# A residual turned partly by 32x32 blocks on VectorE and a gather through DRAM, partly on TensorE

## The chip, the cores and the metric

The kernel runs on one core of a Trainium2 chip. The metric is the device time of one execution in microseconds (us), the median of the runs. Beside it there is one profiled execution, with a trace of every instruction; its span runs from the first instruction of the program to the last. In the views of the profile PE is TensorE, PEld its weight loads, DVE is VectorE, ACT is ScalarE, POOL is GpSimd and SP is SyncE, which here only issues transfers.

## What is computed

One layer of a transformer trunk over 512 tokens of width 2048, in float32. With the depth of 1 only the sliding-window attention mixer is used:

```python
hn = rmsnorm(x, norm_g[0])
y = swa_mixer(hn, swa_w_in[0], swa_w_out[0], swa_sinks[0], rel_bias)   # ends in (out * silu(gate)) @ w_out
x = x + y
emb = p[0] @ ple_proj[0]
g = sigmoid(rmsnorm(x, ple_norm[0]) @ ple_gate[0])
x = x + emb * g
return rmsnorm(x, final_g)
```

Two matrix products of 512x2048 by 2048x2048 matter here: the **output projection** by `w_out`, whose result is added to x, and the **gate product** by `ple_gate`, which takes that new x as its left factor. Between the two, x must be turned: the output projection leaves it with tokens on the 128 partitions, and the gate product needs it with features on the partitions.

## The kernel before

**Number format and pieces.** Every float32 product is made of three passes: each operand is split in a high part (`hi`) and a rest (`lo`) of a narrower type, and `mm3` (lines 126 to 128) issues hi*hi, lo*hi and hi*lo. The weights come in pieces of 128x1024. For each piece SP issues the load of `braw` (line 752), ScalarE casts `bhi` (line 760) and VectorE subtracts to get `blo` (line 761). `Pieces.ahead` splits a piece when TensorE begins on the one two places before it, and the buffers for the split parts are three, so the cast of a piece waits until TensorE has finished the piece three places before it.

**Stages and units.** Each of the two products is done by a scheme of block products that needs fewer multiplications, in six units p, in the order 1, 7, 6, 5, 3, 4, each for two column halves jj. `unit` goes over four pieces m = 0 to 3 of a unit; a piece is 12 matmuls. After each piece come, in this order, some of the list `later` (additions to x, `add_to_x`, lines 1054 and 1056), the calls of `todo` (a step, named (p, jj, m) below), and `between`, which may put the two pieces of a "small" product of 6 matmuls each in between. The last unit of the output projection, p = 4, has small pieces after every step but the last two, two of them after step (4, 1, 0).

**The residual.** `x1[j][:, t, :]` is column block j (of 512) of token block t (of 128). Column blocks 2 and 3 are complete for tokens 256 to 511 after unit 5 and for tokens 0 to 255 after unit 3; column blocks 0 and 1 are complete for tokens 0 to 255 during unit 4 and for tokens 256 to 511 after it.

**The turns.** `turn(kp, th, tag)` turns two of the 16 feature chunks for half of the tokens: four TensorE transposes of 128x128 into one bank of PSUM (line 1038), then two ScalarE multiplications by the norm's weights that write `hT` (line 1041). There are 16 calls, so 64 transposes. Twelve of them stand in the steps of unit 4: 1, 2, 2 and 2 calls in the steps of its first half, and 0, 1, 2 and 2 in those of its second. The first eight (chunks 8 to 15, that is column blocks 2 and 3) take up the first half and step (4, 1, 1). Four more stand in the four steps of (1, 0), the first unit of the gate product.

**The gate product's first operands.** `ple_first`, the forms of unit 1, is four split pairs (lines 865 and 866) of column blocks 2 and 3 for tokens 0 to 255, one made in each step of (4, 1). The forms of unit 7 (lines 858, 870 and 871) also take tokens 256 to 511 of those blocks.

**What sets the order.** In this part of the kernel only TensorE and SP run in the order in which the program is written. VectorE, ScalarE and GpSimd each run in an order that a planner makes when the program is built, from its own costs and from what is ready; it may pull an instruction ahead of its place in the program. From the second unit of the gate product on, all five run in written order. Each engine takes its instructions in its order, one after the other, and waits at one whose input is not there.

**Other names.** `fg` holds the last norm's weights for all partitions (1 MB in SBUF); its load is issued by SP after unit 3 (line 1350). `s1` and `s7` are buffers of 128x2048 that the embedding's products use until step (3, 0, 0) and the gate product from its second half unit on. The tag `e` has two buffers of 128x1024, used by the embedding before and by its loads later.

Of the kernel before, what the change touches and what calls it, by code (L numbers as in the profile page):

```python
# [11 lines left out]
F32 = mybir.dt.float32  # L12
# [6 lines left out]
D = 2048  # L19
S = 512  # L20
P = 128
# [34 lines left out]
def trunk_kernel(ctx: ExitStack, tc: tile.TileContext, a: dict):  # L56
    nc = tc.nc

    def pool(name, bufs=1, **kw):
        return ctx.enter_context(tc.tile_pool(name=name, bufs=bufs, **kw))  # L60
# [9 lines left out]
    pn = const.tile([P, KC], F32, name="pn")  # L70
# [8 lines left out]
    def quarter(name):  # L79
        return whole.tile([P, 4, S], F32, tag="quarter", name=name)  # L80
# [5 lines left out]
    WE = 1024  # L86
# [71 lines left out]
    def run(gen):  # L158
        for _ in gen:
            pass  # L160
# [38 lines left out]
    for k in range(KC):  # L199
# [7 lines left out]
        both = start_pool.tile([P, 2 * 768], F32R, tag="w0s", name=f"w0s{k}")  # L207
# [46 lines left out]
        else:  # L254
            high()
            if k == 1:
                src = xw[:, w_at[512] : w_at[512] + 256]
# [9 lines left out]
        f, e = k == 0, k == KC - 1  # L267
# [18 lines left out]
        for part in "hl" if f else "lh":  # L286
            for t in range(NB):
                c = slice(t * P, (t + 1) * P)
# [6 lines left out]
        if 3 <= k < 3 + NB:  # L295
            t = k - 3
# [104 lines left out]
    for b in range(exact, BUCKETS):  # L401
        d = np.nonzero(bk == b)[0]
        if len(d):
            lo, n = P - 1 + int(d.min()), len(d)
# [301 lines left out]
    for nm, p in SUMS:  # L706
        for q in (6, 5) if (nm, p) == ("ple_gate", 5) else (p,):
            sum_small(nm, q)
        for jj in range(2):
            for m in range(4):  # L710
                t = summed[nm, p, jj, m] = tc.dram_tile([P, WE], F32, name=f"{nm}_{p}_{jj}_{m}")
# [194 lines left out]
    blocks = TWOS * UNITS  # L906
# [64 lines left out]
    late = pool("late", reuse_waits="tile")  # L971
    rooms.append(late)
    x1s = late.tile([P, 4, NB, 512], F32, name="x1s")
    x1 = [x1s[:, j] for j in range(4)]
# [15 lines left out]
    later = []  # L990
# [6 lines left out]
    def unit(p, jj, at, forms, todo, between=lambda m, ps: None):  # L997

        ps = banks(p, jj, forms.nm)
        f = forms.made[p]  # L1000
        first = p not in (6, 5, 3)
        for m in range(4):
            bh, bl = B.get(at[p, jj][m])
            for kk in range(2):
                k = 2 * m + kk
                fh, fl = f[m]
                for tb in range(2):
                    mm3(ps[tb], fh[:, kk, blk(tb)], fl[:, kk, blk(tb)], bh[kk], bl[kk], first and k == 0, k == 7, not first)
            some_later(4 - m)
            todo()  # L1010
            between(m, ps)
        return ps


    def load_x(j, queue):
        queue.dma_start(x1[j], a["x"].rearrange("(t p) d -> p t d", p=P)[:, :, j * 512 : (j + 1) * 512])

    def partial(nm):
        return late.tile([P, 2, 2, 512], F32, tag="partial", name=nm, bufs=3)

    s1, s2, s7 = partial("s1"), partial("s2"), partial("s7")
# [4 lines left out]
    hT, swapped = {}, {}  # L1026

    def turn(kp, th, tag):
# [10 lines left out]
        for n in range(2):  # L1039
            k = 2 * kp + n  # L1040
            nc.scalar.mul(hT[g][:, k % 4, th * 256 : th * 256 + 256], tp[:, n * 256 : n * 256 + 256], pn[:, k : k + 1])

    ple_forms = Forms(swapped, "g")
    ple_first = ple_forms.steps(1)


    missing = {(j, t): {(0, 0): 1, (1, 0): 3, (0, 1): 1, (1, 1): 2}[t // 2, j // 2] for j in range(4) for t in range(NB)}
# [255 lines left out]
    turns = []  # L1303
# [3 lines left out]
    x_at = {(1, 0, 3): 2, (1, 1, 1): 1, (7, 0, 0): 3}  # L1307
    waiting = {(7, 0): (1, 0), (6, 0): (1, 1)}
    held = {}
    for n, p in enumerate(ORDER_OUT):  # L1310
        nxt = out_forms.steps(ORDER_OUT[n + 1]) if n < 5 else iter(())
        for jj in range(2):
            later.extend(held.pop(waiting.get((p, jj)), ()))
            calls = iter(range(4))

            def between(m, ps):
                if (p, jj, m) in EMBED_AT:
                    embedding.slot()
                q = small_steps.get((p, jj, m))
                if q is not None:  # L1320
                    small_out.prepare(q)
                for q in SMALL["w_out"].get((p, jj), {}).get(m, ()):
                    small_out.product(q)

            def todo():
                step = next(calls)
                part = x_at.get((p, jj, step))
                if part is not None:
                    load_x(part, nc.sync)
                part = embed_steps.get((p, jj, step))  # L1330
                if part is not None:
                    embedding.prepare(part)
                next(nxt, None)
                if p == 4:

                    for _ in range({0: 1, 1: 2, 2: 2, 3: 2, 5: 1, 6: 2, 7: 2}.get(4 * jj + step, 0)):
                        turn(*turns.pop(0), "o")
                    if jj:
                        next(ple_first, None)

            ps = unit(p, jj, at_out, out_forms, todo, between)
            posts = [partial_of(add_y, p, jj, tb, ps[tb]) for tb in range(2)]
            if p == 1:
                held[p, jj] = posts
            else:
                later.extend(posts)
        run(nxt)
        if p == 3:
            fg = late.tile([P, D], F32, tag="fg", name="fg")
            nc.sync.dma_start(fg, a["final_g"].partition_broadcast(P))  # L1350
        if p == 3:
            turns = [(kp, th) for kp0, th in ((4, 1), (4, 0), (0, 0)) for kp in range(kp0, kp0 + 4)]
    run(ple_first)
    assert not turns

# [18 lines left out]
    def load_embeds(c, jj):  # L1374
        t = embed_of[c, jj] = late.tile([P, 2, 512], F32, tag="e", name=f"e{c}_{jj}", bufs=2)
        nc.sync.dma_start(t, embeds[c, jj])

    def embeds_for(of, which):
        return {t: embed_of[of, which][:, t % 2] for t in ((2, 3) if of == 5 else (0, 1))}
# [47 lines left out]
    turns = [(kp, 1) for kp in range(4)]  # L1427
# [70 lines left out]
    for n, p in enumerate(ORDER_PLE[:-1]):  # L1498
        if n == 1:

            ctx.enter_context(
                tc.manual_schedule(
                    engines={getattr(mybir.EngineType, v) for v in ("PE", "SP", "DVE", "Activation", "Pool")}
                )
            )
        nxt = ple_forms.steps(ORDER_PLE[n + 1])
        for jj in range(2):
            calls = iter(range(4))

            def todo():  # L1510
                step = next(calls)
                k = early.get((p, jj, step))
                if (p, jj, step) in embed_loads:
                    load_embeds(*embed_loads[p, jj, step])
                while small_due:
                    small_due.pop(0)()
                if (p, jj, step) == (5, 0, 2):
                    assert len(moves) == 4
                    while moves:
                        moves.pop(0)()  # L1520
                if (p, jj, step) == (5, 0, 3):
                    for square in moved.pop(0):
                        square()
                if turns:
                    turn(*turns.pop(0), "t")
                    if not turns:
                        nc.vector.tensor_reduce(ss2, ssq2, axis=AX.X, op=ALU.add)
                        run(power_of_mean(rstd2, ss2, "r2"))
                        nc.scalar.activation(ss2[:, :1], ss2[:, :1], AF.Sigmoid)
                    return  # L1530
                next(nxt, None)
                if p == 1:
                    next(nxt, None)
                if k is not None:
                    split_last(k)
                if (p, jj, step) in opens:
                    open_bank(*opens[p, jj, step])

            def between(m, ps):
                if (p, m) == (7, 3):  # L1540
                    gate(p, jj, ps, None)
                q = ple_steps.get((p, jj, m))
                if q is not None:
                    small_ple.prepare(q)
                for q in SMALL["ple_gate"].get((p, jj), {}).get(m, ()):
                    small_ple.product(q)
                if (p, jj, m) == (6, 1, 1):
                    later.append(partial_of(gate_later, "sum", 0, None, embeds_for(1, 0)))

            ps = unit(p, jj, at_ple, ple_forms, todo, between)  # L1550
            last_two, held_e = (p, jj) == (3, 1), {}
            if not (p == 7 or last_two):
                later.insert(0, partial_of(gate_later, p, jj, ps, held_e))
            for of, which in EMBEDS.get((p, jj), ()):
                e = embeds_for(of, which)
                held_e.update(e)
                if of == 1:
                    later.insert(1, partial_of(gate_later, "sum", which, None, dict(e)))
                    held_e.clear()
            if p == 5:  # L1560
                while moved:
                    later.extend(moved.pop(0))
        run(nxt)
# [4 lines left out]
    f = ple_forms.made[4]  # L1568
# [84 lines left out]
    n = done[3]  # L1653
# [81 lines left out]
```

## Time and profile before

| | |
|---|---|
| median of 3 runs | 787.09 us (786.91 to 787.52) |
| the profiled execution | 787.18 us |
| its span | 785.5 us |
| TensorE clock granted, mean | 0.996 |
| output projection's unit 4, first half | 587.9 to 607.4 us of the span |
| its second half | 607.4 to 624.8 us |
| gate product's first half unit | 624.8 to about 637.9 us |

The table puts the stages by the first TensorE instruction of each in the trace. The profiled execution took 0.09 us more than the median, and 1.7 us of it lie outside the span. A row of a timeline begins with the start and the duration in us, then engine, line, operation, output and inputs; a row of a group ends with the count, the busy time in us, the mean duration of one in ns, and the idle time of the engine before it with what ended it.

### The profile page before, as it was taken

Reading aid. Unit: us, or ns where it says so; the run is one execution under the profiler, and the core shown is the slowest. Engines: PE = TensorE matmul, PEld = TensorE weight load, DVE = VectorE, ACT = ScalarE, POOL = GpSimd, SP = SyncE. Lnnn points to the kernel's source line nnn. Section 1 sums busy time; section 2 is a strip of 40 time slices with the busy share of each in tenths; the row PEclk is TensorE's granted clock in tenths of the full one; section 3 lists DMA queues with packets and bytes.
Section 4 is the critical chain, followed back from the end, with each engine's and each line's share of the span. In section 5 each row is a group of like instructions: output and inputs, shape, how many; then the busy total and the mean of one; then the engine's idle time right before and its main releaser. Section 6 shows DMA issues by size and latency. Waiting matters only on the chain.

```text
span 785.5 us, 11181 instructions
## 1 busy us (share of the span) xinstructions
PE 775.9 (99%) x3700; PEld 648.8 (83%) x3700; DVE 612.1 (78%) x1057; ACT 528.9 (67%) x1121; POOL 149.7 (19%) x273
## 2 busy tenths in 40 slices
PE   9999999999999999999999999999999999999995
PEld 7888888888888888888888888888888888888885
DVE  4547697877877688877878899976897958998996
ACT  6743586766767676766666655678778976667874
POOL 0201423122222314132322200001000002221111
PEclk9999999999999999999999999999999999999998
DMA  9988989999999989999997489868698179999956
GB/s 341 297 210 295 190 251 311 309 287 262 277 265 266 273 235 297 252 302 251 294 252 207 141 318 324 281 204 292 238 374 297 58 298 280 276 280 310 301 116 214
DMA packets 50393, 206.72 MB, mean 263 GB/s; under 512 B 7504, under 2 KB 8528, under 8 KB 44576
## 3 DMA queue, kind: packets, MB, share of 16 engines
q1 hardware_dynamic: 39152, 154.58, 54.9%
q0 software_dynamic: 11184, 51.44, 32.3%
q8 instruction: 29, 0.48, 0.3%
q14 instruction: 28, 0.23, 0.1%
HBM read 192.31 MB, written 75.55 MB: 341 GB/s over the span
## 4 chain that ended last, share of the span: by engine, by line
PE 97%; issue 1%; DMA 0%; DVE 0%; POOL 0%; POOLq 0%; ACT 0%; DVEq 0%; SPq 0%
PE gps L126 7%; PE gps L127 7%; PE gps L128 7%; PE qps L126 7%; PE qps L128 7%; PE qps L127 7%; PE o L127 6%; PE o L128 6%; PE o L126 6%; PE g L128 5%; PE g L127 5%; PE g L126 5%; PE s L485 2%; PE vps L290 2%; PE o L603 2%; PE pt L551 2%
## 5 line engine op out<-in xcount | busy, mean ns | idle before, releaser
L761 DVE TENSOR_TENSOR blo<-braw,bhi 128x1024 fp32r<-128x1024 f32 x100 | 121.9, 1222 | 30.7 <-ACT bhi L760 29.8
L760 ACT CAST bhi<-braw 128x1024 fp32r<-128x1024 f32 x100 | 105.0, 1050 | 39.1 <-PE o L128 15.1
L126 PE MATMUL gps<-xh,whi 128*128 128x512 f32 x256 | 100.0, 390 | 0.0
L127 PE MATMUL gps<-xl,whi 128*128 128x512 f32 x256 | 100.0, 390 | 0.0
L128 PE MATMUL gps<-xh,wlo 128*128 128x512 f32 x256 | 99.8, 390 | 0.0
L126 PE MATMUL qps<-xh,whi 128*128 128x512 f32 x224 | 87.8, 392 | 0.0
L128 PE MATMUL qps<-xh,wlo 128*128 128x512 f32 x224 | 87.5, 390 | 0.0
L127 PE MATMUL qps<-xl,whi 128*128 128x512 f32 x224 | 87.4, 390 | 0.0
L575 POOL TENSOR_SCALAR_AFFINE_SELECT own<-r 64x512 fp32r<-64x512 f32 (+1 forms) x48 | 32.4, 675 | 238.9 <-DVE r L565 235.7
L110 DVE TENSOR_TENSOR wlo<-wraw,whi 128x1024 fp32r<-128x1024 f32 x60 | 73.5, 1227 | 3.4 <-ACT whi L109 3.3
L127 PE MATMUL o<-blo,fho 128*128 128x512 f32 x192 | 74.8, 390 | 0.0
L126 PE MATMUL o<-bhi,fho 128*128 128x512 f32 x192 | 74.8, 390 | 0.0
L128 PE MATMUL o<-bhi,flo 128*128 128x512 f32 x192 | 74.8, 389 | 0.0
L109 ACT CAST whi<-wraw 128x1024 fp32r<-128x1024 f32 x60 | 62.3, 1040 | 5.2 <-issue 4.1
L126 PE MATMUL g<-bhi,fhg 128*128 128x512 f32 x160 | 62.7, 392 | 0.0
L128 PE MATMUL g<-bhi,flg 128*128 128x512 f32 x160 | 62.3, 389 | 0.0
L127 PE MATMUL g<-blo,fhg 128*128 128x512 f32 x160 | 62.3, 389 | 0.0
L128 PEld LDWEIGHTS gps<-xh,wlo 128*128 128x128 f32 x256 | 48.1, 188 | 10.3
L126 PEld LDWEIGHTS gps<-xh,whi 128*128 128x128 f32 x256 | 48.1, 188 | 9.2
L529 ACT ACTIVATE t<-t,sm 128x129 f32<-128x129 f32 (+1 forms) x128 | 49.6, 389 | 8.7 <-DVE sm L525 7.4
L127 PEld LDWEIGHTS gps<-xl,whi 128*128 128x128 f32 x256 | 48.1, 188 | 8.9
L564 ACT CAST r<-pt 128x256 fp32r<-128x256 f32 x56 | 20.8, 372 | 49.9 <-PE pt L551 49.4
(291 smaller groups left out, 1813.2 us busy)
## 6 DMA issues: line engine op xcount, KB each, us to landing
wraw<-in_w_gate_in SPq DMA_DIRECT2D x32, 512.0 KB, 7.7
w_out<-in_w_out POOLq DMA_DIRECT2D x32, 512.0 KB, 9.0
braw<-w_out SPq DMA_DIRECT2D x32, 512.0 KB, 5.4
wraw<-in_w_q SPq DMA_DIRECT2D x28, 512.0 KB, 6.5
braw<-in_w_out SPq DMA_DIRECT2D x22, 512.0 KB, 4.8
braw<-in_ple_gate SPq DMA_DIRECT2D x22, 512.0 KB, 5.8
xw<-in_first SPq DMA_DIRECT2D x14, 640.5 KB, 7.0
w_out<-in_w_out SPq DMA_DIRECT2D x16, 512.0 KB, 10.8
```

Of the source, the lines that this page charges most:

```text
L109: nc.scalar.copy(hi, raw)
L110: nc.vector.tensor_sub(lo, raw, hi.bitcast(F32))
L126: nc.tensor.matmul(ps, sh, mh, start=first, stop=False, skip_group_check=more)
L127: nc.tensor.matmul(ps, sh, ml, start=False, stop=False, skip_group_check=more)
L128: nc.tensor.matmul(ps, sl, mh, start=False, stop=last, skip_group_check=more)
L290: nc.tensor.matmul(v_ps[t], h[:, c], part_of(high_at, 256, 512), start=f, stop=e, skip_group_check=True)
L485: nc.tensor.matmul(s_ps[:, u, : 2 * n], st, of_keys[:, first * 2 * QB : (first * QB + n) * 2], start=True, stop=True)
L529: nc.scalar.activation(su, su, AF.Exp, bias=sm[:, u : u + 1], accum_out=sm[:, 2 + u : 3 + u])
L564: nc.scalar.copy(rh, src)
L575: nc.gpsimd.affine_select(out=flat(own), in_=flat(r).bitcast(F32), pattern=[[0, 8], [sign, HB]], compare_op=ALU.is_ge, fill=0.0, base=-HB ...
L760: nc.scalar.copy(hi[:, :n], raw)
L761: nc.vector.tensor_sub(lo[:, :n], raw, hi[:, :n].bitcast(F32))
```

## The change

Of the 64 transposes, 32 go from TensorE: column blocks 2 and 3 of x, for all tokens. For each of the two blocks and each half of the tokens,

- `turn_blocks` has VectorE turn x by blocks of 32x32, in two instructions of 128x512, into a tile `blocks`, and GpSimd stores the tile (512 KB) to DRAM;
- `gather_blocks` has GpSimd issue four loads of 128 KB, each to 32 partitions, from four places of that DRAM tile, into half of `s1` or `s7`, so that a feature's row comes together;
- `scale_turned` has ScalarE multiply by the norm's weights, in four instructions of 128x256, into `hT`.

`turns_at` places these twelve calls in the steps of unit 4 and of the gate product's first half unit. The remaining eight calls of `turn` (32 transposes) are those of column blocks 0 and 1: four in steps (4, 1, 2) and (4, 1, 3), two in each, and four in the gate product's first half unit, where they were. `ple_first` now goes on after each of the four calls in (4, 1, 2) and (4, 1, 3). The two additions of unit 3's second half to x are put ahead of all else in `later`, as one entry. The load of `fg` stands in step (4, 1, 1) instead of after unit 3.

```diff
+    SQ = P // 4
+    apart, gathered = {}, {}
+
+    def turn_blocks(j, th):
+
+        t = late.tile([P, WE], F32, tag="e", name=f"blocks{j}_{th}", bufs=2)
+        to = t.rearrange("p (a k t q) -> p t k a q", a=4, k=4, t=2)
+        for tb in range(2):
+            assert not missing[j, 2 * th + tb]
+            src = x1[j][:, 2 * th + tb, :].rearrange("p (k a q) -> p k a q", k=4, a=4)
+            nc.vector.transpose(to[:, tb], src)
+        apart[j, th] = tc.dram_tile([P, WE], F32, name=f"apart{j}_{th}")
+        nc.gpsimd.dma_start(apart[j, th], t)
+
+    def gather_blocks(j, th):
+
+        src = apart[j, th].rearrange("(b i) (a x) -> a i b x", b=4, a=4)
+        to = gathered[j, th] = (s7 if th else s1)[:, j % 2].rearrange("p n c -> p (n c)")
+        for quad in range(4):
+            nc.gpsimd.dma_start(to[SQ * quad : SQ * quad + SQ].rearrange("p (b x) -> p b x", b=4), src[quad])
+
+    def scale_turned(j, th):
+
+        if j not in hT:
+            hT[j] = swapped[(j + 2) % 4] = quarter(f"hT{j}")
+        src = gathered[j, th].rearrange("p (b k t q) -> p k b t q", b=4, k=4, t=2)
+        for n in range(4):
+            to = hT[j][:, n, th * 256 : th * 256 + 256].rearrange("p (t b q) -> p b t q", t=2, b=4)
+            nc.scalar.mul(to, src[:, n], pn[:, 4 * j + n : 4 * j + n + 1])
+
+    turns_at = {
+        (4, 0, 0): [(turn_blocks, 2, 0)], (4, 0, 1): [(turn_blocks, 3, 0)],
+        (4, 0, 2): [(gather_blocks, 2, 0), (turn_blocks, 2, 1)], (4, 0, 3): [(gather_blocks, 3, 0), (turn_blocks, 3, 1)],
+        (4, 1, 0): [(gather_blocks, 2, 1)], (4, 1, 1): [(scale_turned, 2, 0), (gather_blocks, 3, 1)],
+        (4, 1, 2): [(scale_turned, 3, 0)],
+        (1, 0, 1): [(scale_turned, 2, 1)], (1, 0, 3): [(scale_turned, 3, 1)],
+    }
...
                 if p == 4:
-
-                    for _ in range({0: 1, 1: 2, 2: 2, 3: 2, 5: 1, 6: 2, 7: 2}.get(4 * jj + step, 0)):
+                    turns_due((p, jj, step))
+                if (p, jj, step) == (4, 1, 1):
+                    fg = late.tile([P, D], F32, tag="fg", name="fg")
+                    nc.sync.dma_start(fg, a["final_g"].partition_broadcast(P))
+                if (p, jj) == (4, 1):
+                    for _ in range(2 if step >= 2 else 0):
                         turn(*turns.pop(0), "o")
-                    if jj:
                         next(ple_first, None)
...
             if p == 1:
                 held[p, jj] = posts
+            elif (p, jj) == (3, 1):
+                later.insert(0, lambda both=posts: [post() for post in both])
             else:
                 later.extend(posts)
         run(nxt)
         if p == 3:
-            fg = late.tile([P, D], F32, tag="fg", name="fg")
-            nc.sync.dma_start(fg, a["final_g"].partition_broadcast(P))
-        if p == 3:
-            turns = [(kp, th) for kp0, th in ((4, 1), (4, 0), (0, 0)) for kp in range(kp0, kp0 + 4)]
+            turns = [(kp, 0) for kp in range(4)]
...
+                if p == 1:
+                    turns_due((p, jj, step))
                 if turns:
                     turn(*turns.pop(0), "t")
```

More of the change, by code (lines that the diff above doesn't have):

```diff
@@ L1041, in turn, with turns_due @@
             nc.scalar.mul(hT[g][:, k % 4, th * 256 : th * 256 + 256], tp[:, n * 256 : n * 256 + 256], pn[:, k : k + 1])
+    SQ = P // 4
[28 more added lines that the diff above has]
+    }
+    def turns_due(at):
+        for part, j, th in turns_at.get(at, ()):
+            part(j, th)
     ple_forms = Forms(swapped, "g")
@@ L1309, in trunk_kernel @@
     held = {}
+    fg = None
     for n, p in enumerate(ORDER_OUT):
@@ L1325, in todo @@
             def todo():
+                nonlocal fg
                 step = next(calls)
```

## The prediction, made before the changed kernel was built or run

> **What bounds the kernel now.** I read the page's busy shares first, then its chain of work that ended last, then the table of windows for the three stretches that the change touches, and last the timelines inside them.
>
> ```profile
> span 785.5 us, 11181 instructions
> PE 775.9 (99%) x3700; PEld 648.8 (83%) x3700; DVE 612.1 (78%) x1057; ACT 528.9 (67%) x1121; POOL 149.7 (19%) x273
> PE 97%; issue 1%; DMA 0%; DVE 0%; POOL 0%; POOLq 0%; ACT 0%; DVEq 0%; SPq 0%
> ```
>
> TensorE is busy for 99% of the span and is 97% of the chain. So whatever leaves TensorE's queue shortens the run, if no other engine then keeps it waiting. The windows say how near the others are (us, then busy us and instructions of PE, PEld, DVE, ACT, POOL, then clock, DMA share, GB/s):
>
> ```profile
> 587.90:607.40 19.50, 19.50 (x101) 16.39 (x100) 14.66 (x17) 16.11 (x31) 0.00 (x0) 1.00 0.82 305
> 607.40:624.80 17.40, 17.40 (x88) 14.28 (x86) 15.79 (x18) 16.09 (x31) 0.00 (x0) 1.00 0.15 55
> 624.80:637.50 12.70, 12.70 (x66) 10.49 (x64) 7.64 (x11) 10.90 (x22) 1.05 (x1) 1.00 0.54 204
> ```
>
> These are the first half of unit 4, its second half, and nearly all of the gate product's first half unit. TensorE has no gap in any. VectorE is busy for 75%, 91% and 60%, ScalarE for 83%, 92% and 86%; GpSimd has next to nothing to do, and the DMA engines are at 15% in the second stretch. The reader is to see that TensorE is the bound by a small margin only.
>
> **What leaves TensorE.** The duration of a transpose is not its price, since matmuls overlap. I take the distance from start to start:
>
> ```profile
> 577.71 0.39 PE L126 MATMUL o<-bhi,fho 128*128 128x512 f32 x1
> ...
> 590.41 0.39 PE L128 MATMUL o<-bhi,flo 128*128 128x512 f32 x1
> 590.64 0.60 PE L1038 MATMUL tp<-ident,x1s 128*128 128x128 f32 x4
> ...
> 595.21 1.03 PE L1038 MATMUL tp<-ident,x1s 128*128 128x128 f32 x8
> ...
> 600.21 1.03 PE L1038 MATMUL tp<-ident,x1s 128*128 128x128 f32 x8
> ...
> 605.19 1.03 PE L1038 MATMUL tp<-ident,x1s 128*128 128x128 f32 x8
> ...
> 610.15 0.39 PE L126 MATMUL smallo<-bhi,small_aho 128*128 128x512 f32 x1
> ...
> 615.79 0.60 PE L1038 MATMUL tp<-ident,x1s 128*128 128x128 f32 x4
> ...
> 620.36 1.03 PE L1038 MATMUL tp<-ident,x1s 128*128 128x128 f32 x8
> ```
>
> From 577.71 to 590.41 are 56 steps, so a matmul takes 0.227 us of the queue. Between the start of one group of transposes and the next stand 18 matmuls (a small piece of 6 and a piece of 12), 4.08 us. The intervals are 4.57, 5.00, 4.98 and 4.96 us, and 4.57 for the group at 615.79; what is over 4.08 is 0.49, 0.92, 0.90, 0.88 and 0.49 us. These five groups are the 32 transposes that go: **3.68 us**. The groups from 620.36 on are the 32 that stay, so they cancel.
>
> [...]
>
> One wait goes too, the only one on the chain in these stretches:
>
> ```profile
> 613.15 0.50 PE L127 MATMUL o<-blo,fho 128*128 128x512 f32 x1
> 613.49 0.39 PE L128 MATMUL o<-bhi,flo 128*128 128x512 f32 x1
> 610.73 2.05 ACT L760 CAST bhi<-braw 128x1024 fp32r<-128x1024 f32 x2
> 610.74 1.23 DVE L858 TENSOR_TENSOR hT<-hT 128x1024 f32<-128x1024 f32 x1
> 611.88 2.35 DVE L761 TENSOR_TENSOR blo<-braw,bhi 128x1024 fp32r<-128x1024 f32 x2
> ```
>
> A `blo` was late because VectorE was doing a subtraction for unit 7 of the gate product, pulled some 30 us ahead of its place by the planner. The next start came 0.34 us on, not 0.23: 0.1 us. After the change this subtraction's input (tokens 256 to 511, scaled in (1, 0)) does not exist yet, so it cannot be there. It also shows what is late next: here the lead is two small pieces, 2.7 us, and cast and subtraction take 1.0 and 1.2 us in series.
>
> **What VectorE gets.** Eight block turns of 128x512. No row of this trace shows this operation. The nearest rows are the other 128x512 instructions of VectorE and, as the upper end, twice the width:
>
> ```profile
> 578.77 0.68 DVE L1054 TENSOR_TENSOR x1s<-smallo,x1s 128x512 f32<-128x512 f32 x1
> 579.37 0.68 DVE L1100 TENSOR_TENSOR small_alo<-gate,small_aho 128x512 fp32r<-128x512 f32 x1
> ...
> 591.01 0.68 DVE L1100 TENSOR_TENSOR small_alo<-small_sums_o,small_aho 128x512 fp32r<-128x512 f32 x1
> L761 DVE TENSOR_TENSOR blo<-braw,bhi 128x1024 fp32r<-128x1024 f32 x100 | 121.9, 1222 | 30.7 <-ACT bhi L760 29.8
> ```
>
> One takes 0.60 us from start to start, one of 1024 elements 1.14 to 1.22. I take 0.60 (same number of elements, type and memory), so 4.8 us in all, and keep 1.2, so 9.6 us, as the other end; below 0.60 I see no reason, since none of the 128x512 rows is shorter.
>
> All eight lie in the first half of unit 4, which shrinks from 19.5 to about 16.3 us. VectorE's work there becomes 14.66 + 4.8 = 19.5 us. The 3.1 us too much can pass into the second half, where of 15.79 us the two early subtractions (2 x 1.14) go and the time becomes 16.9 us: 3.4 us are free. So over both halves VectorE is all but full. Piece by piece, in written order, I get each `blo` ready 0.4 to 1.6 us before TensorE wants it. At the third piece of (4, 0), for one: VectorE is through with the row at 591.01 by 591.6, then come two turns (1.2), a `blo` (1.14), an addition (0.60) and this `blo` (1.14), done at 595.7; TensorE wants it 24 matmuls after 590.64, at 596.1. The second small piece of (4, 1) and the piece after it have 0.4 and 0.5. With 0.4 us as the smallest lead and two turns in a row being 1.2 us, the planner's order will not always fit. I charge **0.6 us** of waits for late `blo` (0 to 1.5).
>
> **What ScalarE gets.** 16 multiplications of 128x256 out of PSUM go, 16 out of SBUF come:
>
> ```profile
> L1041 ACT ACTIVATE hT<-tp,pn 128x256 f32<-128x256 f32 x32 | 12.8, 470 | 0.0
> L376 ACT CAST V<-values 128x256 fp32r<-128x256 f32 x4 | 1.6, 398 | 2.4 <-DVE values L388 2.4
> 620.00 0.61 ACT L870 CAST fhg<-hT 128x512 fp32r<-128x512 f32 x1
> 623.64 1.12 ACT L870 CAST fhg<-hT 128x512 fp32r<-128x512 f32 x2
> 637.50:651.00 13.50, 13.50 (x62) 11.22 (x61) 7.42 (x7) 8.33 (x11) 0.00 (x0) 1.00 0.97 361
> ```
>
> 0.40 us each on either side, so the sum is nothing; but they move. The 14 in the first half of unit 4 (5.6 us) leave it, which helps the casts there. Eight come into (4, 1) for two that go, and eight into (1, 0). The second half then asks 16.09 + 6 x 0.4 = 18.5 us of ScalarE in 16.9 us, less the three casts for unit 7 at 620.00 and 623.64, which were early and can wait, 1.7 us: full. In (1, 0) it is 10.90 + 3.2 = 14.1 us in 12.7; what is left over falls into the next half unit, whose 8.33 us become some 10 in 13.5. The casts of pieces stand ahead of the scaling in written order, with 4 us and more of lead there, so I charge nothing more than 0.1 us for it; without that cover it would be up to 3 us.
>
> **What the transfers get.** Four stores of 512 KB and sixteen loads of 128 KB on GpSimd's queue:
>
> ```profile
> 560.68 0.53 POOL L1245 DMA_DIRECT2D embeds<-made  x1 [3.80 <-ACT made L1256]
> 628.88 1.05 POOL L1366 TENSOR_TENSOR rstd<-ms_r,power 128x4 f32<-128x4 f32 x1 [67.67 <-DVE ms_r L1364]
> L739 POOL DMA_DIRECT2D grown<-in_ple_gate x16 | 14.0, 874 | 62.8 <-DVE blo L761 41.6 <-DMA grown<-ple_gate 21.3
> embeds<-made POOLq DMA_DIRECT2D x8, 512.0 KB, 4.3
> bias<-tdram SPq DMA_DIRECT2D x32, 20.0 KB, 11.3
> fg<-in_final_g SPq DMA_DIRECT2D x1, 1024.0 KB, 7.3
> 579.29 0.38 SPq L1350 DMA_DIRECT2D fg<-in_final_g  x1
> 600.56 0.43 SPq L752 DMA_DIRECT2D braw<-in_ple_gate  x1
> 620.31 0.33 SPq L752 DMA_DIRECT2D braw<-in_ple_gate  x1
> ```
>
> GpSimd is empty from 561 to 628 us, so the 20 issues (0.53 to 0.87 us, 11 to 17 us) delay nobody but each other. A store like this lands in 4.3 us; for the loads of 1 KB rows I take 5 us and keep 11.3 us, that of the small-row loads, as the far end. With the turns of block 2 done by about 592.5 us: store landed by 597, its loads issued by 601 and landed by 606; the store of the second tile of block 2 follows in the queue, then the loads of block 3 from 603 to 607, landed by 612. In written order ScalarE reaches the scalings at about 611 and 615 us, so the data is there 3 to 5 us before. The forms that need it are wanted by TensorE at 621 and 627. For tokens 256 to 511 the last load lands by about 621 and is wanted at 625 to 631.
>
> Moving the `fg` load: SP runs far ahead of TensorE, so in its queue the load will come just before that of the gate product's first weights at 600.56, not at 610. These are cast at about 617, and between them and 620 SP issues nothing; 1 MB, 7.3 us to landing, is hidden, and costs up to 3 us without that. The same gap takes the 4 MB of stores and loads. Putting unit 3's additions first moves two instructions that VectorE already did at that place: nothing.
>
> **Sum.** -3.7 (transposes) -0.1 (the wait) +0.6 (VectorE) +0.1 (ScalarE) = **-3.1 us**. From the profiled execution's 787.18 us that is 784.1; the median is 0.09 below that execution, well inside the spread, and I leave it. Under 0.2%, 1.6 us, a measurement of this kernel does not tell from no change.
>
> **The rivals.**
>
> ```profile
> 585.00:590.00 5.00, 5.00 (x24) 4.14 (x23) 5.00 (x8) 3.63 (x7) 0.00 (x0) 1.00 1.01 408
> ```
>
> *VectorE becomes the bound* (0.17). If a turn takes 1.2 us, its eight are 9.6 us, and the two halves ask 14.66 + 9.6 + 13.5 = 37.8 us of VectorE in 33.2 us of TensorE. Some 2 us of work can be late at the end and wait (form splits, additions); 2.6 us are waited for: -3.8 + 2.6 = -1.2, so **786.0**, the same. For it: VectorE is full already as unit 4 begins (third busy time of the row). Against: all its 512-wide rows are at 0.60. [...]
>
> *A gather that lands late stops ScalarE* (0.11, the slower side). ScalarE waits at the first multiplication of `scale_turned`, and the casts of pieces queue behind it. With 11.3 us for each landing and 1 us an issue, block 3's loads are out by 613 and land at 624 instead of 612, while ScalarE is there at 615: 9 us, less some 4 us of pieces split ahead, is a wait of 5.4 us for TensorE, and -3.8 + 5.4 = +1.6, so **788.8** and more. The point from which it costs is a landing past 619 us; from about 622.5 it eats the gain. The planner can make it likelier by putting the scaling ahead of casts. Against: the DMA engines are at 15% there, and the embeds' stores landed in 4.3 us.
>
> *The time comes back as small waits* (0.06): ScalarE over-full in (4, 1) and (1, 0), 1.5 us each, and VectorE's 0.6: about **787.0**, the same. That the transposes were never on the path is excluded by the chain's own share.
>
> **Chances and range.** The forecast has 0.66, all of it faster by over 0.2%; the two rivals at 786.0 and 787.0 give 0.23 for the same; 0.11 for slower. The forecast's own range is 783.3 (all 3.8 us and no wait) to 785.2. The range goes to 787.2, which takes in the same-side rivals and leaves out the slower one; its low end is 783.2.
>
> **What would show it.** 32 transposes on TensorE, none before (4, 1, 2), and unit 4 taking about 33.2 + 0.7 us instead of 36.9. Block turns of 0.6 to 0.7 us. Waits of TensorE or its weight loads for `blo` of under 1 us in total. No wait of ScalarE for the loads into `s1` and `s7`. The prediction is wrong if a turn takes over 1 us, if such a wait shows, or if anything after 640 us differs.

## The result, and the profile after

| | before | after |
|---|---|---|
| median of 3 runs, us | 787.09 (786.91 to 787.52) | 791.96 (791.42 to 791.98) |
| the profiled execution, us | 787.18 | 791.96 |
| its span, us | 785.5 | 790.2 |
| TensorE clock granted, mean | 0.996 | 0.992 |

The ratio of the two times is 1.0059, with an interval of 1.0036 to 1.0081. The change makes the kernel 4.9 us slower; the prediction was 784.1 us, 7.9 us lower, and the time lies outside its range (783.2 to 787.2).

The page of the changed kernel, in the three lines that were shown first for the kernel before:

```profile
span 790.2 us, 11162 instructions
PE 776.3 (98%) x3668; PEld 647.2 (82%) x3668; DVE 616.4 (78%) x1065; ACT 528.3 (67%) x1121; POOL 162.8 (21%) x293
PE 84%; issue 10%; DMA 3%; POOL 1%; ACT 1%; DVE 0%; POOLq 0%; DVEq 0%; ACTq 0%
```

TensorE has 32 instructions fewer and yet 0.4 us more of busy time, so some of them became longer. Its share of the chain falls from 97% to 84%, and DMA, which had none, is on it. The chain itself, in order of time (start, length, what), shows where:

```profile
577.42 7.88 DMA apart<-blocks
585.30 0.28 issue
585.58 1.38 POOL s L1062 x3
586.96 0.29 issue
587.25 0.55 POOL s L1062
587.81 13.60 issue
...
601.42 4.01 DMA apart<-blocks
...
609.02 10.05 DMA s<-apart
...
620.08 0.95 ACT bhi L760
...
621.05 1.24 DVE blo L761
```

The chain goes through the new path: a store, GpSimd's issue of the loads, a load of 10.05 us, then ScalarE's cast and VectorE's subtraction of a piece that has nothing to do with the load. The view of waits (engine, line, releaser: us in total, times, longest) says who stood, first for TensorE, then for ScalarE and VectorE:

```profile
PE smallo L126 <- ACT bhi L760: 2.9, 1, 2.9
PE o L127 <- DVE blo L761: 1.0, 2, 0.8
PE smallo L127 <- DVE blo L761: 0.5, 1, 0.5
ACT hT L1071 <- DMA s<-apart: 8.7, 2, 5.7
DVE blocks L1053 <- DMA apart<-blocks: 1.7, 1, 1.7
```

The wait whose absence the prediction named as a sign is there: ScalarE stood 8.7 us, in two goes, at the first multiplication of `scale_turned`, for the loads. The timeline of ScalarE around the first of them (the bracket is the idle time before the row):

```profile
588.90 0.62 ACT L1024 ACTIVATE s<-x1s 128x512 f32<-128x512 f32 x1
589.43 0.18 ACT L1024 ACTIVATION_READ_ACCUMULATOR s<-x1s 128x1 f32 x1
595.27 1.30 ACT L1071 ACTIVATE hT<-s,pn 128x256 f32<-128x256 f32 x3 [5.65 <-DMA s<-apart]
596.48 1.03 ACT L760 CAST bhi<-braw 128x1024 fp32r<-128x1024 f32 x1
```

ScalarE reaches the scaling of block 2 at 589.6 us, not at 611: the planner has pulled it some 20 us ahead of its written place, in front of the cast at 596.48. GpSimd's timeline has the store and the loads that it waits for:

```profile
577.42 0.54 POOL L1055 DMA_DIRECT2D apart<-blocks  x1 [16.37 <-DVE blo L761]
585.58 2.22 POOL L1062 DMA_DIRECT2D s<-apart  x4 [7.62 <-DMA apart<-blocks]
601.42 0.56 POOL L1055 DMA_DIRECT2D apart<-blocks  x1 [13.61 <-DVE blocks L1053]
```

The store of block 2 leaves at 577.4, 15 us before the 592.5 of the prediction, since its two turns were pulled ahead too; it takes 7.9 us, and the loads land at 595.2, 9.6 us after the first was issued. The two windows below (us, then busy us and instructions of PE, PEld, DVE, ACT, POOL, then clock, DMA share, GB/s) show the stretch in which they land, and how the clock stood a little later:

```profile
585.00:595.00 10.00, 9.71 (x43) 7.70 (x41) 6.98 (x9) 3.57 (x6) 2.22 (x4) 1.00 1.02 326
600.00:604.00 4.00, 4.00 (x11) 3.13 (x10) 4.00 (x6) 2.50 (x5) 0.56 (x1) 0.50 0.88 252
```

The DMA engines are full in the first (share 1.02). In the second TensorE is busy throughout, with 11 matmuls where 4 us hold 17 or 18 at 0.227 us: the granted clock is 0.50. TensorE's timeline around its wait:

```profile
591.83 0.39 PE L126 MATMUL o<-bhi,fho 128*128 128x512 f32 x1
...
594.32 0.39 PE L128 MATMUL o<-bhi,flo 128*128 128x512 f32 x1
597.57 0.80 PE L126 MATMUL smallo<-bhi,small_aho 128*128 128x512 f32 x1 [2.86 <-ACT bhi L760]
598.83 0.80 PE L127 MATMUL smallo<-blo,small_aho 128*128 128x512 f32 x1 [0.47 <-DVE blo L761]
599.42 0.63 PE L128 MATMUL smallo<-bhi,small_alo 128*128 128x512 f32 x1
...
604.11 0.47 PE L127 MATMUL o<-blo,fho 128*128 128x512 f32 x1
...
605.34 0.40 PE L126 MATMUL smallo<-bhi,small_aho 128*128 128x512 f32 x1
...
616.23 0.39 PE L126 MATMUL o<-bhi,fho 128*128 128x512 f32 x1
...
624.96 1.03 PE L1038 MATMUL tp<-ident,x1s 128*128 128x128 f32 x8
```

From 591.83 to 605.34 TensorE issues two pieces and a small one, 30 matmuls, 6.80 us at 0.227; it takes 13.51, so 6.71 us are lost. About 3.3 of them are the two waits in brackets. The rest, 3.4 us, goes with the half clock: the 11 steps of 0.427 us from 599.42 to 604.11 are 2.2 of it, and most of what is left lies at the two matmuls right behind the waits, which take 0.80 us each. From 604.42 on the steps are about 0.23 again.

A second, smaller loss follows: from 616.23 to 624.96 are 30 matmuls again, in 8.73 us, so 1.9 us are lost. Of these, 1.3 lie from 620.7 to 622.7, behind ScalarE's second wait, 3.05 us before 619.17 for block 3's loads. The other 0.5 comes at 616.89, too early for that wait: there a `blo` is late because VectorE does two splits of `ple_first` first (line 866, 1.29 us from 613.82). The second wait hangs in part on the first: VectorE, standing 5.4 us for the cast, came to the second turn of block 3 only at 600.42, so that tile's store left at 601.4; in e1 below, without the first wait, it left at 596.1.

The two losses are together 8.6 us; less the 3.78 us that the prediction takes off (3.68 of transposes and 0.1 of the old wait) that is 4.9 us, what was measured. No other group of matmuls of these stages lost over 0.2 us by itself.

### The profile page after: what moved, and what is told of

Its sections match the earlier page's. It is cut to its first block, busy times and chain, and to the rows that moved or that the text cites. A ratio compares the mean times of both kernels' runs of the same rounds, so it can differ in the third digit from the quotient of the medians.

```text
span 790.2 us, 11162 instructions
## 1 busy us (share of the span) xinstructions
PE 776.3 (98%) x3668; PEld 647.2 (82%) x3668; DVE 616.4 (78%) x1065; ACT 528.3 (67%) x1121; POOL 162.8 (21%) x293
## 4 chain that ended last, share of the span: by engine, by line
PE 84%; issue 10%; DMA 3%; POOL 1%; ACT 1%; DVE 0%; POOLq 0%; DVEq 0%; ACTq 0%
PE gps L126 7%; PE gps L127 7%; PE gps L128 7%; PE qps L126 7%; PE qps L128 7%; PE qps L127 7%; PE g L128 5%; PE g L126 5%; PE g L127 5%; PE o L127 3%; PE o L126 3%; PE o L128 3%; PE s L485 2%; PE vps L290 2%; PE o L603 2%
## 5 line engine op out<-in xcount | busy, mean ns | idle before, releaser
L565 DVE TENSOR_TENSOR r<-pt,r 128x256 fp32r<-128x256 f32 x56 | 23.7, 424 | 38.8 <-ACT r L564 38.0
```

Of the source, the lines that this page charges most:

```text
L565: nc.vector.tensor_sub(rl, src, rh.bitcast(F32))
```

## The experiments

All times are medians; a ratio is against the kernel before on the same chip.

**e1_hold: the scaling kept behind the casts.** The planner gets an order for `scale_turned`: not before the last cast of a piece that is written ahead of it.

```diff
-            nc.scalar.copy(hi[:, :n], raw)
+            self.last_cast = nc.scalar.copy(hi[:, :n], raw)
...
-            nc.scalar.mul(to, src[:, n], pn[:, 4 * j + n : 4 * j + n + 1])
+            with tc.issue_after(B.last_cast.ins):
+                nc.scalar.mul(to, src[:, n], pn[:, 4 * j + n : 4 * j + n + 1])
```

> The changed kernel with one difference: each scaling of a gathered block is held in ScalarE's queue behind the last cast of a weight piece that stands before it in the program, so the planner can no longer put it there before its loads have landed. Theory (ScalarE stands at a scaling whose loads have not landed, the casts behind it come late, TensorE runs dry and then goes on at half clock): the 5.7 us wait of ScalarE at 589.6 us goes, TensorE's 2.9 us idle and the slow stretch after it go, 783.5 to 785.5 us in all. Rival (VectorE's block turns make the split parts late): nothing changes for VectorE, 789 us or more. Rival (4 MB of extra transfers slow the weights): 789 us or more.

Measured: 786.34 us (784.78 to 789.97, 10 runs), ratio 0.9993 (0.998 to 1.0005). In ScalarE's timeline of this kernel the scalings stand where the prediction put them, and neither waits:

```profile
612.36 1.69 ACT L1072 ACTIVATE hT<-s,pn 128x256 f32<-128x256 f32 x4
613.96 1.99 ACT L760 CAST bhi<-braw 128x1024 fp32r<-128x1024 f32 x2
616.48 1.69 ACT L1072 ACTIVATE hT<-s,pn 128x256 f32<-128x256 f32 x4
```

So the place of the scaling is what made ScalarE stand: by the medians, 5.6 us of the 8.6 come back. That is still 0.8 us above what was expected, and the runs spread over 5 us. In the profiled execution (785.38 us, 1 us below the median) what is left is another wait, of VectorE, from its view of waits and its timeline:

```profile
DVE blocks L1053 <- DMA apart<-blocks: 2.1, 1, 2.1
DVE hT L858 <- ACT hT L1072: 1.6, 2, 0.9
```
```profile
601.90 0.71 DVE L1053 STREAM_TRANSPOSE blocks<-x1s 128x512 f32<-128x512 f32 x1 [2.06 <-DMA apart<-blocks]
602.54 2.32 DVE L761 TENSOR_TENSOR blo<-braw,bhi 128x1024 fp32r<-128x1024 f32 x2
```

The tag `e` has two buffers and there are four tiles `blocks`: a tile may be written only when the store of the tile two before it has landed. Here it is the fourth tile, and the store of the second one, issued at 596.1. VectorE stands at the turn, and the subtractions for `blo` queue behind it; TensorE lost 0.8 us there and 1.0 us after 634 us, where the forms of unit 7 (second line) and those of a small product came late.

**e2_no_wait: the scaling without the loads as its input.** The scalings read x itself, so the gate product gets its column blocks 2 and 3 unturned; turns, stores and loads all stay.

```diff
-        src = gathered[j, th].rearrange("p (b k t q) -> p k b t q", b=4, k=4, t=2)
+        src = x1[j][:, 2 * th : 2 * th + 2, :].rearrange("p u (v b t q) -> p (u v) b t q", v=2, b=4, t=2)
```

> The changed kernel, but the scalings read x itself instead of the gathered blocks, so they wait for no load; the block turns, the stores and the loads are all still done, and nothing uses the loads (what the gate product gets is x unturned). Theory (ScalarE's wait for the loads): 783.3 to 785 us, the full 3.7 us of transposes less under 1.5 us of small waits. Rival (VectorE) and rival (transfers): both are still there in full, 789 us or more.

Measured: 786.4 us (785.15 to 789.27), ratio 0.9997 (0.9986 to 1.0007). The expectation was missed by over 1 us: with ScalarE free of the loads the time is that of e1, and VectorE stands 2.0 us at a turn here too. The first wait is worth the same whether its cause or its place is taken away, and something else remains.

**e3_hold_twice: e1 with every block turn done twice.**

```diff
-            nc.vector.transpose(to[:, tb], src)
+            for _ in range(2):
+                nc.vector.transpose(to[:, tb], src)
```

> The first kernel of this call with every block turn done twice, 16 instead of 8 instructions of 0.7 us on VectorE. If VectorE is as full as I reckoned (its work in unit 4 about equal to TensorE's), the further 5 us give 2 to 4 us over the first kernel. If VectorE were already what makes the changed kernel late, 5 us and more over it. If VectorE has room, under 1 us over it.

Measured: 794.17 us (793.46 to 795.12), ratio 1.0089 (1.0074 to 1.0104). It does not tell what it was made for, which was whether VectorE has time for more turns (the first kernel of the expectation is e1): the planner set the turns differently, and VectorE now stood 5.7 us for a store. TensorE's timeline has 6.61 us of idle time behind that:

```profile
615.16 0.80 PE L127 MATMUL smallo<-blo,small_aho 128*128 128x512 f32 x1 [6.61 <-DVE blo L761]
```

**e4_only_added: the kernel before with all its 64 transposes, and the turns, stores and loads beside them, their data unused.** The `fg` load is where it was; the scalings are not there. Unit 3's additions stand first, as in the changed kernel.

```diff
+                    turns_due((p, jj, step))
...
+    turns_at = {
+        (4, 0, 0): [(turn_blocks, 2, 0)], (4, 0, 1): [(turn_blocks, 3, 0)],
+        (4, 0, 2): [(gather_blocks, 2, 0), (turn_blocks, 2, 1)], (4, 0, 3): [(gather_blocks, 3, 0), (turn_blocks, 3, 1)],
+        (4, 1, 0): [(gather_blocks, 2, 1)], (4, 1, 1): [(gather_blocks, 3, 1)],
+    }
```

> The kernel before with all 64 transposes kept on TensorE, and beside them, with nothing that uses their result, the eight block turns, the four stores and the sixteen loads (the last norm's weights load where they did). Theory (only the wait for the loads costs): 787 us, within 1 us of the kernel before. Rival (VectorE's turns): 789 to 791 us. Rival (transfers): 789 to 791 us.

Measured: 790.64 us (790.08 to 792.14), ratio 1.0046 (1.0031 to 1.0061). The expectation was missed: this was 3.4 us over the kernel before, where the two rivals had put it, with no ScalarE in it that could wait for a load. But the wait of VectorE for the store, seen in e1 and e2, is here without ScalarE's, in VectorE's timeline and then in TensorE's:

```profile
603.01 0.71 DVE L1053 STREAM_TRANSPOSE blocks<-x1s 128x512 f32<-128x512 f32 x1 [4.36 <-DMA apart<-blocks]
603.65 1.18 DVE L761 TENSOR_TENSOR blo<-braw,bhi 128x1024 fp32r<-128x1024 f32 x1
```
```profile
604.89 0.50 PE L127 MATMUL o<-blo,fho 128*128 128x512 f32 x1 [2.33 <-DVE blo L761]
```

By the distance of starts TensorE lost 2.6 us there and 0.75 us more at another late `blo` at 616 us. That made a new theory, to be set against the rivals: two waits, ScalarE's for the loads and VectorE's for the store that frees a buffer.

**e5_hold_own: e1, and a place of their own for the second two tiles.** They go into the space of `fg`, and the `fg` load moves on to step (1, 0, 3).

```diff
+        if th:
+            if "own" not in apart:
+                apart["own"] = late.tile([P, D], F32, tag="fg", name="blocks_own")
+            t = apart["own"][:, (j - 2) * WE : (j - 1) * WE]
+        else:
+            t = late.tile([P, WE], F32, tag="e", name=f"blocks{j}_{th}", bufs=2)
```

> The held kernel of before, and beside it buffers of their own for the blocks of tokens 256 to 511 (the space of the last norm's weights, whose load moves to step (1, 0, 3)), so that VectorE never stands at a block turn until a store has landed. Theory now (two waits of the same kind, ScalarE's for the loads and VectorE's for a store, each in front of a weight piece): both are gone, TensorE waits under 0.5 us in unit 4, 783.3 to 784.8 us, and the spread of the runs becomes small. Rival (VectorE has no time for the turns themselves): still 785.5 us or more. Rival (transfers slow the weights): still 785.5 us or more.

Measured: 784.8 us (784.24 to 784.84), ratio 0.9967 (0.9954 to 0.998). Neither wait is left, TensorE has no gap in unit 4, and the runs lie within 0.6 us of each other, where those of e1 spread over 5. With both repairs the change gives a gain of 0.2% to 0.46%, and the time is 0.7 us above the forecast. Those 0.7 have a place: 1.0 us between 634 and 642 us is lost as in e1, where ScalarE is late with the scalings in (1, 0).

**e6_added_own: e4 with the own buffers** (and so with the `fg` load at step (1, 0, 3), as in e5).

> The kernel that only adds turns, stores and loads to all 64 transposes on TensorE, now with buffers of their own for the blocks of tokens 256 to 511. Theory: the 3.4 us that the addition cost were VectorE's wait for a store, so it comes to within 0.8 us of the kernel before, 786.7 to 787.9 us. Rivals (the turns' time on VectorE, the transfers): still 789 us or more.

Measured: 787.5 us (787.22 to 788.18), ratio 1.0004 (0.9994 to 1.0013). The 3.4 us of e4 are gone. Eight turns, four stores and sixteen loads beside the full work of the kernel before cost nothing that can be measured; only the wait for a buffer did. The moved `fg` load is not what helped: in e10, where it stands after unit 3 as in e4, it was issued at 579.4 us and took 9.0 us, so it had landed by 588.4; VectorE's wait in e4 lasted from 598.65 to 603.01.

**e7_no_wait_own: e2 with the own buffers** (the gate product gets x unturned, as there).

> The kernel whose scalings read x itself (the gate product gets x unturned), now with buffers of their own as well: neither wait is left, but all turns, stores and loads are done. Theory: 783.0 to 784.5 us. Rivals (turns on VectorE, transfers): 785.5 us or more.

Measured: 784.41 us (783.6 to 784.66), ratio 0.9962 (0.9948 to 0.9977), as the two waits ask: without them, 2.7 us below the kernel before, by another way than e5.

**e8_own: the changed kernel with the own buffers alone, the scalings where the planner puts them.**

> The changed kernel with buffers of their own alone, the scalings where the planner puts them. Theory: ScalarE's wait for the loads of the first block stays and with it TensorE's idle time and the half clock after it, so about 6 us over the held kernel with such buffers: 788 to 791 us. If the store's wait were the only one that matters, 783.5 to 785 us.

Measured: 795.84 us (793.91 to 797.4), ratio 1.0108 (1.0088 to 1.0128): slower than the changed kernel, where I had expected 788 to 791. With the buffers free the planner pulls more of the work ahead, and ScalarE stands three times; its view of waits and its timeline:

```profile
ACT hT L1076 <- DMA s<-apart: 13.1, 3, 5.7
```
```profile
573.66 1.30 ACT L1076 ACTIVATE hT<-s,pn 128x256 f32<-128x256 f32 x3 [4.74 <-DMA s<-apart]
...
596.91 1.31 ACT L1076 ACTIVATE hT<-s,pn 128x256 f32<-128x256 f32 x3 [2.71 <-DMA s<-apart]
...
619.98 0.91 ACT L1076 ACTIVATE hT<-s,pn 128x256 f32<-128x256 f32 x2 [5.67 <-DMA s<-apart]
```

e5 differs from it in the hold alone: 11 us. Of the two repairs the hold is the one without which the other does harm.

**e9_early: e5 with tokens 256 to 511 first, and their scalings in unit 4.**

```diff
+        (4, 0, 0): [(turn_blocks, 2, 1)], (4, 0, 1): [(turn_blocks, 3, 1), (gather_blocks, 2, 1)],
+        (4, 0, 2): [(gather_blocks, 3, 1), (turn_blocks, 2, 0)], (4, 0, 3): [(scale_turned, 2, 1), (turn_blocks, 3, 0)],
+        (4, 1, 0): [(gather_blocks, 2, 0), (scale_turned, 3, 1)], (4, 1, 1): [(gather_blocks, 3, 0), (scale_turned, 2, 0)],
+        (4, 1, 2): [(scale_turned, 3, 0)],
```

> e5_hold_own with the turns, loads and scalings of tokens 256 to 511 put first, in the steps of unit 4, and their scalings at (4, 0, 3) and (4, 1, 0) instead of (1, 0, 1) and (1, 0, 3); the planner still keeps each scaling behind the last cast before it. Theory: what e5 has left, 1.0 us between 634 and 642 us, is ScalarE late with the forms of unit 7 and the small product because the eight scalings (3.4 us) stand in (1, 0); in unit 4 ScalarE has that time free, and the loads for these tokens had landed by about 584 us in e5. Expected 783.3 to 784.2 us, no wait of TensorE of over 0.1 us between 590 and 645 us. Rival: the scaling meets loads that have not landed yet, since their order on GpSimd's queue changes, and ScalarE stands again in unit 4: then 786 to 790 us and a wait of ScalarE for the loads of over 2 us. Second rival: the forms of unit 7 are late for another reason (additions to x, the table load), and the time stays at 784.8.

Measured: 784.45 us (784.03 to 784.63), ratio 0.9962 (0.9948 to 0.9975). The 1.0 us after 634 us is gone, so it did hang on the scalings in (1, 0). But ScalarE has now more to do in unit 4, and one `blo` there is late; TensorE's view of waits:

```profile
PE o L127 <- DVE blo L761: 0.3, 1, 0.3
```

By the distance of starts that piece lost 0.62 us. The time is 0.25 us above what was expected and can't be told from e5's. e5 and e9 are the versions that beat both kernels and still compute the whole layer.

**e10_fg_back: the changed kernel with the `fg` load after unit 3 again.**

```diff
+        if p == 3:
+            fg = late.tile([P, D], F32, tag="fg", name="fg")
+            nc.sync.dma_start(fg, a["final_g"].partition_broadcast(P))
...
-                if (p, jj, step) == (4, 1, 1):
-                    fg = late.tile([P, D], F32, tag="fg", name="fg")
-                    nc.sync.dma_start(fg, a["final_g"].partition_broadcast(P))
```

> The changed kernel with one thing undone: the last norm's weights load after unit 3 again, where the kernel before has it, instead of step (4, 1, 1). Question: does the moved 1 MB, issued at 604.4 us of the changed kernel's trace, lengthen the landing of block 3's loads (10.0 us from 609.0) and so ScalarE's second wait? If the move costs nothing, as predicted: 791.4 to 792.4 us, and ScalarE's two waits for the loads stay at about 5.7 and 3.0 us. If the second wait hangs on it: up to 1.9 us less, 790.0 to 790.6, with the second wait of ScalarE gone or under 1.5 us. Rival: the 1 MB then lies beside block 2's store and loads, whose landing gets longer still, and the first wait grows: 793 us and more.

Measured: 792.01 us (791.19 to 792.59), ratio 1.0062 (1.0045 to 1.0078), as the changed kernel. ScalarE's second wait is 2.06 us instead of 3.05 in the one profile, its first 5.75; the time does not show it.

## Why the prediction was wrong

**The step that failed** is the one on the transfers: "In written order ScalarE reaches the scalings at about 611 and 615 us, so the data is there 3 to 5 us before." It rests on two things, and both were off.

- *The order.* The section on the kernel before says that ScalarE's order is the planner's, which may pull an instruction ahead, and the prediction showed it doing so with a subtraction some 30 us early. Yet the step took the written order, for the turns (592.5 us; the store left at 577.4) and for the scalings (611 us; 589.6). With the order held (e1) the scalings are at 612.4 and 616.5 and wait for nothing.
- *The landing.* The columns of the view of DMA issues are kind, count, size and median us to landing:

```profile
apart<-blocks POOLq DMA_DIRECT2D x4, 512.0 KB, 8.6
s<-apart POOLq DMA_DIRECT2D x16, 128.0 KB, 8.0
fg<-in_final_g SPq DMA_DIRECT2D x1, 1024.0 KB, 11.0
```

  I took 4.3 us from the `embeds` stores, between 514 and 561 us with the DMA engines at 0.48 to 0.95 by windows of 10 us, and 5 us as an estimate, and set the 15% DMA share of (4, 1) against the rival. But moved ahead, block 2's transfers fall into a stretch whose own row, quoted in the prediction for VectorE's sake, had the DMA engines at 1.01, and they took 7.9 and 9.6 us. With 4.3 and 5 us the last of them, issued some 2 us after the store's landing, would have been there by about 588.7, 0.9 us ahead of the 589.6 at which ScalarE came. By this estimate it took both errors to make the first wait; that the order alone, put right, removes it is what e1 shows, and the landing alone was not run.

**The rival that came true** is *a gather that lands late stops ScalarE*, which had 0.11. Its mechanism is what happened, and it named the planner's pull as what would make it likelier. Its place was half right: block 3's loads landed at 619.1, the point from which it said that it costs, and that was the smaller wait; block 2's was not priced. Its price was too low, 788.8 against 791.96: 5.4 us of lost time were allowed, 8.6 were lost. Of these, 3.4 us go with the halved clock after the first wait, which no step had, and 0.5 are not ScalarE's wait but a `blo` that VectorE made late.

**A wait that was not on the list** is VectorE's for a store, through the two buffers of `e`. The prediction went by the turns' time and did not ask when the tile they write comes free. In the changed kernel it was 1.7 us with little behind it, hidden by the larger one; where ScalarE does not stand, the kernel is 3.4 us longer with it (e4) than without it (e6, within 0.4 us of the kernel before). That is why taking the first wait away gave only 786.3.

The other terms, one by one:

- *The transposes, -3.7, and the old wait, -0.1:* right. e5 is 2.7 us of span below the kernel before (782.8 against 785.5), with 1.0 us of waits still in it: 3.7.
- *The block turn, 0.60 us from start to start, and the rival VectorE becomes the bound:* the price was right, the rival is out. In the changed kernel's view of groups:

```profile
L1053 DVE STREAM_TRANSPOSE blocks<-x1s x8: 669/705/712, 574.3 to 610.4; 128x512 f32<-128x512 f32 x8
```

  0.70 us each, 0.02 us more than the 128x512 rows it was taken from; two in a row take 1.30 us, so 0.60 from start to start, half of the 1.2 us that the rival took. e6 shows that they cost nothing where no buffer is waited for.
- *VectorE's 0.6 us of late `blo`:* 0.5 in the changed kernel (at 616.89), 0 in e5, 0.6 in e9. A fair size for a term that hangs on the order.
- *ScalarE's 0.1 us:* too small. With the transfers out of the way (e5), its overfull (1, 0) costs 1.0 us, which the prediction had seen as 14.1 us of work in 12.7 and then covered by lead. This is the third rival, the time as small waits, in a small way.
- *The `fg` load, nothing:* right within the measurement (e10), though it landed in 11.0 us rather than 7.3.

The sum of the forecast, then, fits kernels without the two waits: 784.1 against 784.8 (e5) and 784.45 (e9). That it fits so well is in part luck: in e5 the 0.6 us for VectorE came out as 0 and the 0.1 us for ScalarE as 1.0, and the two errors nearly cancel.

What stays open: why the planner puts the scaling so early (that it takes a transfer to be shorter than 8 to 10 us is argued; its costs were not changed in any run), and how much VectorE's time for the turns would cost alone, since e3 mixed it with the store's wait.

## What to carry to other kernels

Where a planner orders an engine, an input that comes by DMA must be priced at the place to which the planner can pull its reader, not where it is written, and with the landing time of the busiest stretch that it can be pulled into (here 7.9 us for the store and 9.6 us for the loads, where 4.3 and 5 were taken); a reader that other work queues behind is best tied after that work. When work moves to an idle engine, ask for each tile that it writes when the tile's last reader, a store included, lets it go (VectorE stood 1.7 us for one in the changed kernel and 4.4 us in e4). And a wait of TensorE can cost more than its length: in the changed kernel 3.3 us of waits cost 6.7, with the half clock that followed.

## What the runs showed of the hardware

In four places of the traces the granted clock was at half beside a short idle stretch of TensorE, and stayed there for some time after TensorE worked again:

- In the changed kernel the idle stretch was 2.86 us. By windows of 0.25 us the clock was 0.50 from 597.4 us, 2.7 us after the end of TensorE's last matmul, to 604.2, so for 6.8 us.
- In e3 it was 6.61 us. The clock was 0.50 in the windows from 612 to 617 us and 0.75 in the next, of 2 us; from 618.17 on the steps were 0.23 us again.
- In e8 there were two, of 1.61 and 0.75 us, with a single matmul between. The three windows of 2 us from 576 to 582 had 0.82, 0.50 and 0.82, about 3.4 us if that was one stretch at 0.50.
- Later in e8 TensorE's view of waits has one of 3.0 us for a cast; ScalarE had stood for loads until 619.98 us, and the windows from 622 to 628 all had 0.50.

At an idle stretch of 2.33 us in e4 the clock did not fall: the windows from 602 to 608 us had 1.00. Windows of e8, after the two shorter stretches, and of e4, from 0.9 us before TensorE works again:

```profile
578.00:580.00 2.00, 2.00 (x6) 1.52 (x6) 1.86 (x3) 2.00 (x5) 0.00 (x0) 0.50 1.03 244
```
```profile
604.00:606.00 2.00, 1.11 (x5) 0.94 (x6) 2.00 (x3) 0.00 (x0) 1.95 (x5) 1.00 0.98 303
```
